# Ordering VectorE and GpSimd work by its room in dry runs, in a hybrid attention and retention layer

## The chip, the cores and the metric

The kernel runs on one core of a Trainium2 chip. The metric is the device time of one execution in microseconds, as the median of the runs taken. Engines are named as in the profile: PE is TensorE (matmuls, with its weight loads as PEld), DVE is VectorE, ACT is ScalarE, POOL is GpSimd, SP is SyncE, which here issues the DMAs. Each engine carries out its own instructions strictly in the order in which the program emits them, and waits on semaphores for the others.

## The reference, cut to what matters

One decoder layer on a sequence of 1024 tokens, model width 1024, float32. Two token mixers read one input projection: retention with 8 heads, in chunks of 128 tokens, and a sparse attention with 8 query heads on one shared key and value, in which an indexer scores all earlier keys for each query and keeps the best 256. Their outputs go through one output projection; a gated convolutional MLP (inner width 2816) follows.

```python
def reference(x, ...):
    hn = rms_norm(h, mix_norm_pre[l])
    proj = hn @ w_in[l]
    rq, rk, rv, rg, aq, ak, av, iq, ik, iw = split_columns(proj)
    ...
    ret_out = retention(rq, rk, rv, rg)
    ...
    att_out = dsa_attention(aq, ak, av, iq, ik, iw)
    mixed = jnp.concatenate([ret_out, att_out], axis=-1) @ w_out[l]
    h = h + rms_norm(mixed, mix_norm_post[l])
    hn = rms_norm(h, ffn_norm_pre[l])
    up = causal_dwconv(hn @ w_up[l], conv_w[l], conv_b[l])
    g, u = jnp.split(up, 2, axis=-1)
    ffn = (jax.nn.silu(g) * u) @ w_down[l]
    h = h + rms_norm(ffn, ffn_norm_post[l])
```

## The kernel before, in words

The sequence is cut into eight query tiles of 128 tokens (t, or block b in attention). Every float32 matrix product is made of three matmuls on rounded halves: an operand is split into a high half (a cast, mostly on ScalarE) and a low half (a subtraction on VectorE or GpSimd). Up and down projection use a scheme of seven block products in place of eight, numbered i = 0, 1, ..., with operands that are sums of blocks.

What sets the order is a planner inside the program. Each piece of work is a generator (a task) that yields operations, events to wait for, and requests for buffers; the class `Flow` steps them. `Lane` stands for an engine and estimates an operation's length (`cost`), and how long VectorE and GpSimd hold the SBUF port that they share (`port`). `Flow.run` (L308) takes the engine on which some waiting operation can start first, and on that engine the operation with the smallest estimated start plus patience times priority (patience 0 for PE, 0.02 for ScalarE, 0.001 for VectorE, 0.005 for GpSimd); ties go to the smaller priority number. Where an operation may run on several engines, the one that ends it first by the estimates takes it. The operation is emitted at once, so the planner's order is the program's order on each engine. `Store` hands out buffers (pages, PSUM banks) in the same estimated time.

```python
    def run(self):
        ...
            for k in self.live:
                op = k.ops[0] if len(k.ops) == 1 else min(k.ops, key=lambda o: self.start(k, o) + o.us + o.lane.bias)
                ways.append((self.start(k, op), k.prio, k.seq, k, op))
            lane = min(ways, key=lambda w: w[:3])[4].lane
            start, _, _, k, op = min((w for w in ways if w[4].lane is lane),
                                     key=lambda w: (w[0] + lane.patience * w[1], w[1], w[2]))
            self.live.remove(k)
            op.emit()
```

The tasks that matter here, in the program's order. `projections` (L873) runs the input projection's columns over pairs of tiles; each finished tile of columns 0 to 3 starts a `ret_unit` (L902, retention for two heads and one tile: rotations on GpSimd, small matmuls, decay on VectorE), the last column starts `aq_post` (L994, the rotation of the attention queries, on GpSimd) and `att_queries` (L1007). `search` (L801) finds each query's threshold by bisection, followed by a selection chain on VectorE (compare, scan, multiply) for each tile. `att_pair` (L1049) makes a block's logits for two heads; `softmax` (L1078) takes maximum (VectorE), exponential (ScalarE), reciprocal (VectorE or GpSimd) and scaling (GpSimd, ScalarE or VectorE); then PE transposes the probabilities and multiplies them with the values. `w_split` (L483) splits weights of the output projection, whose matmuls are `mix0` and `mix1`; `mix1_post` (L1171), `hn_part` (L1233) and `hn_pair` (L1244) normalise its result and prepare sums of blocks for the up projection, `up_first` (L1309) and `up_sums` (L1334) its first operands. In the down projection `dn_split` (L1525, priority 25) splits the operands (product i, step k, side j) and `dn_sums` (L1563, priority 24) makes the sums that products 2, 3 and 5 need. All matmuls are recorded at L437, transposes at L447, loads at L407.

## Time and profile before

| | us |
|---|---|
| median of 3 runs (1332.53 to 1333.96) | 1333.94 |
| the profiled execution | 1332.06 |
| its span | 1330.3 |
| TensorE busy | 1256.3 |
| VectorE busy | 1085.3 |
| ScalarE busy | 715.9 |
| GpSimd busy | 362.8 |

The profiled execution took 1332.06 us, of which 1330.3 are the span, from the first to the last instruction on the profile; the other 1.8 lie around it. The mean granted clock of TensorE is 0.983 of full speed. Busy time is what instructions of an engine covered; waiting inside the span is the rest. The views used below are tables of busy time by window and timelines of one engine, in which the idle time ahead of an instruction stands in brackets with what ended it.

### The profile page before, as it was taken

The page shows a single profiled execution, that of the slowest core. Times are in us where ns is not written, and L with a number is a line of the kernel's source. Part 1 is how long each engine was busy: PE and PEld are TensorE (multiplying, and loading weights), DVE is VectorE, ACT ScalarE, POOL GpSimd, SP SyncE. Part 2 cuts the span into 40 slices and gives each one's busy share as a digit, 9 for nine tenths or more (in the row PEclk, how much of TensorE's full clock was granted, in tenths as well). Part 3 has the DMA queues.
Part 4 walks back from the last instruction along what each step waited for, and adds up shares of the span by engine and source line. Part 5 has one row for each costly group of instructions (what it writes and reads, how often), then busy time and mean ns, then how long its engine had stood idle before and what let it go on. Part 6 is the DMA issues. An engine that isn't in the chain of part 4 may idle for free.

```text
span 1330.3 us, 17741 instructions
## 1 busy us (share of the span) xinstructions
PE 1256.3 (94%) x6058; PEld 1031.2 (78%) x6058; DVE 1085.3 (82%) x1968; ACT 715.9 (54%) x1511; POOL 362.8 (27%) x524
## 2 busy tenths in 40 slices
PE   8899999999987999999799999999999999899997
PEld 6787888888865888887577787777787778678876
DVE  7895898898888888858889987787787677896766
ACT  6685687787546778844445544434444435344440
POOL 4864475675798323114300000000000000000001
PEclk9999999999998999999899999999999999899999
DMA  7100010120202000033213332222121329542335
GB/s 239 48 17 24 8 57 25 40 58 8 68 0 64 1 1 14 28 142 111 96 50 133 102 96 78 65 95 80 64 95 64 103 68 357 201 143 79 119 117 192
DMA packets 54811, 111.47 MB, mean 84 GB/s; under 512 B 6592, under 2 KB 8256, under 8 KB 54720
## 3 DMA queue, kind: packets, MB, share of 16 engines
q1 hardware_dynamic: 54720, 110.33, 24.9%
q8 instruction: 48, 0.79, 0.3%
q14 instruction: 43, 0.35, 0.1%
HBM read 90.38 MB, written 19.92 MB: 83 GB/s over the span
## 4 chain that ended last, share of the span: by engine, by line
PE 75%; DVE 9%; POOL 7%; ACT 4%; issue 3%; DMA 2%; SPq 0%; DVEq 0%; POOLq 0%; ACTq 0%
PE big L437 38%; PE bank L437 34%; DVE page L136 4%; POOL wide L136 4%; PE bank L447 3%; DVE wide L136 3%; ACT page L136 2%; DVE BIG L136 1%; POOL sms L136 1%; ACT wide L136 1%; PE big L447 1%; POOL page L136 0%; DMA wide<-in_w_dn 0%; DMA wide<-glu_scratch 0%; POOL osq L136 0%
## 5 line engine op out<-in xcount | busy, mean ns | idle before, releaser
L437 PE MATMUL big<-page,BIG 128*128 128x512 f32 x984 | 256.4, 406 | 1.2 <-DVE BIG L136 1.0
L136 DVE TENSOR_TENSOR page<-page,page 128x512 fp32r<-128x512 f32 (+3 forms) x321 | 220.2, 719 | 15.6 <-ACT page L136 12.8
L437 PEld LDWEIGHTS big<-page,BIG 128*128 128x128 f32 x984 | 180.8, 189 | 36.9 <-DVE BIG L136 1.2
L437 PE MATMUL big<-page,page 128*128 128x512 f32 (+4 forms) x797 | 191.8, 376 | 15.1 <-DVE page L136 9.4
L437 PEld LDWEIGHTS big<-page,page 128*128 128x128 f32 x797 | 140.9, 189 | 46.2 <-DVE page L136 11.3
L437 PE MATMUL bank<-page,page 128*128 128x512 f32 (+1 forms) x767 | 168.0, 363 | 2.5 <-ACT ajunk L136 1.3
L437 PE MATMUL bank<-page,BIG 128*128 128x512 f32 (+2 forms) x696 | 156.9, 371 | 3.9 <-DVE BIG L136 2.0
L437 PEld LDWEIGHTS bank<-page,page 128*128 128x128 f32 x767 | 132.4, 192 | 25.1 <-DVE page L136 1.9
L136 POOL TENSOR_SCALAR ss<-ss 128x1 f32<-128x1 f32 x8 | 4.2, 519 | 501.6 <-ACT ajunk L136 501.2
L437 PE MATMUL big<-BIG,page 128*128 128x512 f32 x516 | 131.4, 403 | 9.9 <-ACT page L136 4.7
L437 PEld LDWEIGHTS bank<-page,BIG 128*128 128x128 f32 x696 | 119.8, 197 | 20.8 <-ACT BIG L136 3.1
L437 PE MATMUL bank<-BIG,page 128*128 128x512 f32 x540 | 132.6, 395 | 0.0
L437 PEld LDWEIGHTS big<-BIG,page 128*128 128x128 f32 x516 | 97.3, 191 | 38.0 <-ACT page L136 7.8
L136 DVE SCALAR_TENSOR_TENSOR page<-page,convp,page 128x1023 f32<-128x1023 f32 x86 | 110.0, 1280 | 13.5 <-ACT page L136 12.6
L437 PEld LDWEIGHTS bank<-BIG,page 128*128 128x128 f32 x540 | 101.0, 188 | 24.2
L136 DVE TENSOR_SCALAR_CACHE_REDUCE wide<-page,cand 128x384 bf16<-128x384 f32 (+5 forms) x136 | 111.5, 820 | 2.8
L136 ACT CAST page<-page 128x512 fp32r<-128x512 f32 x146 | 87.3, 619 | 42.2 <-PE bank L437 12.5
L136 POOL TENSOR_TENSOR wide<-wide,page 128x128 f32<-128x128 f32 (+3 forms) x153 | 105.1, 709 | 15.7 <-ACT wide L136 13.5
L136 ACT ACTIVATE page<-page,convp 128x1024 f32<-128x1024 f32 x43 | 53.5, 1244 | 90.4 <-PE big L437 38.2
L437 PE MATMUL big<-wide,page 128*128 128x512 f32 x396 | 96.3, 391 | 1.5 <-DVE page L136 0.8
L437 PE MATMUL bank<-wide,page 128*128 128x512 f32 x396 | 95.9, 391 | 0.0
L136 DVE TENSOR_TENSOR page<-bank,page 128x512 fp32r<-128x512 f32 (+3 forms) x111 | 70.5, 638 | 29.2 <-PE bank L437 16.1
(184 smaller groups left out, 2003.7 us busy)
## 6 DMA issues: line engine op xcount, KB each, us to landing
page<-in_w_up SPq DMA_DIRECT2D x88, 256.0 KB, 3.3
glu_scratch<-page SPq DMA_DIRECT2D x21, 512.0 KB, 2.9
wide<-in_w_main SPq DMA_DIRECT2D x40, 256.0 KB, 2.7
wide<-glu_scratch SPq DMA_DIRECT2D x26, 256.0 KB, 5.4
BIG<-glu_scratch SPq DMA_DIRECT2D x25, 256.0 KB, 3.4
BIG<-in_w_dn SPq DMA_DIRECT2D x24, 256.0 KB, 3.9
wide<-in_w_dn SPq DMA_DIRECT2D x22, 256.0 KB, 5.8
page<-in_w_dn SPq DMA_DIRECT2D x20, 256.0 KB, 3.9
```

The costliest lines, as they stand in the source:

```text
L136: return lambda *a, **kw: Op(self, self.cost(m, a, kw), lambda: f(*a, **kw), port=self.port(m, a, kw))
L437: x = nc.tensor.matmul(o, l, r, start=st, stop=sp_, skip_group_check=more)
L447: x = nc.tensor.transpose(tr[:, j * P:(j + 1) * P], s, ident)
```

## The change

The program now plans its order up to twelve times without emitting anything, and emits the order of the best. Each dry run logs every operation with its start, its engine, its end, the operations on which it depends and a key that names it in every run. `Flow.latest` goes back from the end and gives each operation the latest moment at which it can start without delaying what depends on it or the next operation of PE. In the following run `Flow.rank` takes the place of patience times priority on VectorE and GpSimd: an operation's room is its latest moment minus its present start, and what is added to the start in the comparison is 0.3 us for 30 us of room or more, and less in proportion below that. The plan handed on is the mean of the last one and the new one. In the order that comes out as best, a plan is in use; it holds the same operations as before.

Two estimates are corrected: a matmul whose moving operand is in the buffer `BIG` counts 2195 columns for each us in place of 2240, and the scan on VectorE now holds the port that VectorE and GpSimd share. Since tasks may now overtake each other, some buffers are given back only after more events (`att_end`, `up_rest`, `mix1_post`, the rotation table, the controller).

```diff
+PASSES = 12
...
-        if self.name != "dve" or "accum_out" in kw or m in ("memset", "tensor_tensor_reduce", "tensor_tensor_scan"):
+        if self.name != "dve" or "accum_out" in kw or m in ("memset", "tensor_tensor_reduce"):
...
+    def rank(self, lane, w):
+
+
+        if not self.plan or lane.name not in ("dve", "pool"):
+            return lane.patience * w[1]
+        room = self.plan.get(w[3].key + (-1, w[3].calls), w[0] + 20.0) - w[0]
+        return 0.3 * min(1.0, max(0.0, room / 30.0))
+
+    def latest(self):
+
+        end = max(r[2] for r in self.log)
+        late = [end] * len(self.log)
+        after = end
+        for n in sorted(range(len(self.log)), key=lambda n: -self.log[n][0]):
+            start, lane, ready, deps, _ = self.log[n]
+            x = min(late[n], after) if lane == "pe" else late[n]
+            late[n] = x = x - (ready - start)
+            if lane == "pe":
+                after = x
+            for d in deps:
+                late[d] = min(late[d], x)
+        return {r[4]: late[n] for n, r in enumerate(self.log)}
...
-                                     key=lambda w: (w[0] + lane.patience * w[1], w[1], w[2]))
+                                     key=lambda w: (w[0] + self.rank(lane, w), w[1], w[2]))
             self.live.remove(k)
-            op.emit()
+            if not self.dry:
+                op.emit()
...
+            n = len(self.log)
+            self.log.append((start, op.lane.name, k.ready, k.deps, k.key + (-1, k.calls)))
+            k.calls += 1
+            k.deps = (n,)
...
-            us += max(0.11, n / 2240) if r.dtype == F32R else 2 * max(0.107, n / 1200) + 0.0053
+            us += max(0.11, n / (2195 if "BIG" in str(r.name) else 2240)) if r.dtype == F32R else 2 * max(0.107, n / 1200) + 0.0053
...
+        flow.set(turned[c, t])
...
+        if b in (3, 5):
+            yield R_ev[3, T - 1]
...
-        if t == T - 1:
+        left[0] -= 1
+        if not left[0]:
             mem.put(gp, g2)
...
+                yield ev[2]
...
-        for e in aq_ev:
+        for e in aq_ev + list(turned.values()):
...
-        yield att_ev[T - 1]
+        for e in att_ev:
+            yield e
...
+    if dry:
+        raise Ordered(flow, not any(s.queue for s in (mem, acc, bigs)))
...
+    def build(plan, dry):
+        nc = _bacc.Bacc("TRN2", target_bir_lowering=False, num_devices=1, dynamic_dma_scratch_size=1024)
+        io = {k: nc.dram_tensor(f"in_{k}", v.shape, mybir.dt.from_np(v.dtype), kind="ExternalInput").ap()
+              for k, v in arrays.items()}
+        out = nc.dram_tensor("out_0", (S, D), F32, kind="ExternalOutput").ap()
+        with tile.TileContext(nc) as tc:
+            hybrid_layer(tc, io, out, plan, dry)
+        return nc
+
+    best, plan, ends = {}, {}, []
+    for i in range(PASSES):
+        try:
+            build(plan, True)
+        except Ordered as run:
+            if not run.whole:
+                break
+            end = max(r[2] for r in run.flow.log)
+            if not ends or end < min(ends):
+                best = plan
+            ends.append(end)
+            late = run.flow.latest()
+            plan = {k: 0.5 * (plan.get(k, t) + t) for k, t in late.items()}
+    nc = build(best, False)
```

How it moves instructions is shown at three pieces. The first is TensorE, in attention, up to the transposes of the probabilities of block 1, heads 4 and 5. In these rows `ident` is the identity of a transpose, `page_394` and `page_395` hold keys (the matmuls on them are logits), matmuls with `BIG` in groups of three are steps of a projection or of `mix0`. Before (the transposes of heads 4 and 5 are the last two rows):

```order
L437 MATMUL big_4024<-page_395,page_3677 128x256
L447 MATMUL bank_4021<-ident,wide_91 128x128 x4
L447 MATMUL bank_4056<-ident,page_4002 128x128 x4
L447 MATMUL bank_4063<-ident,wide_91 128x128 x4
L447 MATMUL bank_4066<-ident,page_4002 128x128 x4
L437 MATMUL bank_4057<-page_4030,page_296 128x256 x4
L437 MATMUL big_4085<-page_394,page_4001 128x384
L437 MATMUL big_4085<-page_395,page_4001 128x384
L437 MATMUL big_4090<-page_394,page_4001 128x384
L437 MATMUL big_4090<-page_395,page_4001 128x384
L447 MATMUL bank_4125<-ident,wide_91 128x128
L447 MATMUL bank_4125<-ident,page_3958 128x128
```

After (the transposes of heads 4 and 5 are again the last two rows):

```order
L485 MATMUL big_3957<-page_394,page_3669 128x256
L485 MATMUL big_3957<-page_395,page_3669 128x256
L485 MATMUL big_3921<-page_2859,BIG 128x512 x3
L485 MATMUL bank_3968<-page_3422,BIG 128x512 x3
L485 MATMUL big_3921<-page_3294,BIG 128x512 x6
L485 MATMUL big_3921<-page_3311,BIG 128x512 x6
L495 MATMUL bank_4000<-ident,wide_91 128x128 x4
L485 MATMUL big_4013<-page_394,page_3899 128x384
L485 MATMUL big_4013<-page_395,page_3899 128x384
L485 MATMUL big_3921<-page_3325,BIG 128x512 x6
L495 MATMUL bank_4026<-ident,page_3887 128x128
L495 MATMUL bank_4026<-ident,page_3888 128x128
```

Ahead of these transposes now stand seven projection steps and one of `mix0` (x3 is one step, x6 two), where before the last projection step lay further up and only transposes and attention's own matmuls stood; the logits of block 2 come one pair instead of two ahead of them.

The second piece is VectorE in the same place. ISA with `mxs` is the maximum of a softmax and the read of its accumulator; SCALAR_TENSOR_TENSOR with `wide` alone is the selection's scan. Before (block 1, head 4 is the maximum on `big_3959`; the scan is that of tile 7):

```order
L136 TENSOR_SCALAR wide_91<-page_1291,cand 128x1024
L136 TENSOR_TENSOR page_3895<-wide_89,page_3895 128x512
L136 SCALAR_TENSOR_TENSOR wide_89<-wide_91 128x1024
L136 SCALAR_TENSOR_TENSOR wide_91<-wide_89,cnt,wide_91 128x1024
L136 TENSOR_TENSOR page_3957<-bank_3951,page_3957 128x256
L136 ISA wide_91,mxs<-big_3959,wide_89 128x256
L136 ISA mxs 128x1
L136 SCALAR_TENSOR_TENSOR page_1291<-page_1291,cand,wide_91 128x1024
```

After (head 4 is the maximum on `big_3897`, heads 5 to 7 those that follow; the scan is that of tile 6, and the RECIPROCAL is head 4's):

```order
L138 ISA page_3887,mxs<-big_3897,wide_89 128x256
L138 ISA mxs 128x1
L138 TENSOR_TENSOR page_3913<-bank_3891,page_3913 128x512
L138 ISA page_3888,mxs<-big_3907,wide_89 128x256
...
L138 ISA wide_89,mxs<-big_3938,wide_89 128x256
...
L138 ISA wide_91,mxs<-big_3957,wide_89 128x256
...
L138 SCALAR_TENSOR_TENSOR wide_91<-wide_90 128x896
L138 RECIPROCAL sms<-sms 128x1
```

The scan of tile 7 and the selection around it stood ahead of head 4's maximum; now the maxima of all of block 1 stand ahead of tile 6's scan, and tile 7's comes later still. Head 4's reciprocal, which was on GpSimd behind the rotations of tiles 6 and 7, follows the scan of tile 6 on VectorE.

The third piece is VectorE at the start of the down projection, around the low halves of product 0, steps 9 and 10. Before, these are the rows on `page4_9591` and `page5_9613` (step 9) and `page12_9637` and `page7_9640` (step 10); those on `page6_9614` and `page20_9636` belong to product 1, and the rest are `dn_sums`:

```order
L136 TENSOR_TENSOR BIG_9369<-page14_8946,page0_9048 128x512
L136 TENSOR_TENSOR page0_9048<-wide0_9366,page11_9046 128x512
L136 TENSOR_TENSOR BIG_9369<-BIG_9369,page15_8801 128x512
L136 TENSOR_TENSOR page4_9591<-wide2_9368,page4_9591 128x512
L136 TENSOR_TENSOR BIG_9369<-BIG_9369 128x512
L136 TENSOR_TENSOR page5_9613<-wide2_9368,page5_9613 128x512
L136 TENSOR_TENSOR page15_8801<-page15_8801,wide0_9366 128x512
L136 TENSOR_TENSOR page6_9614<-wide2_9368,page6_9614 128x512
L136 TENSOR_TENSOR page0_9048<-BIG_9369,page14_8946 128x512
L136 TENSOR_TENSOR page20_9636<-wide2_9368,page20_9636 128x512
L136 TENSOR_TENSOR page12_9637<-wide1_9367,page12_9637 128x512
L136 TENSOR_TENSOR page7_9640<-wide1_9367,page7_9640 128x512
```

After, they are the rows on `page17_9608` and `page0_9630` (step 9) and `page12_9653` and `page1_9661` (step 10):

```order
L138 TENSOR_TENSOR BIG_9385<-page1_9392,page20_8955 128x512
L138 TENSOR_TENSOR page17_9608<-wide1_9383,page17_9608 128x512
L138 TENSOR_TENSOR BIG_9385<-BIG_9385,page20_8955 128x512
L138 TENSOR_TENSOR BIG_9385<-wide0_9382 128x512
L138 TENSOR_TENSOR BIG_9385<-page1_9392,BIG_9385 128x512
L138 TENSOR_TENSOR page0_9630<-wide1_9383,page0_9630 128x512
L138 TENSOR_TENSOR page20_8955<-page20_8955,page13_9386 128x512
L138 TENSOR_TENSOR BIG_9385<-wide1_9383,page5_8813 128x512
L138 TENSOR_TENSOR page20_8955<-page1_9392 128x512
L138 TENSOR_TENSOR BIG_9385<-BIG_9385,page8_8814 128x512
L138 TENSOR_TENSOR page12_9653<-wide0_9382,page12_9653 128x512
L138 TENSOR_TENSOR page1_9661<-wide0_9382,page1_9661 128x512
```

The sums among these rows are now those of steps 0 and 1 and before were those of steps 2 and 3: the four low halves have moved ahead of most of `dn_sums`.

## Rows read from the trace of the kernel before

**Rows 1.** The page, part 1: each engine's busy time, its share of the span, and its instructions.

```profile
PE 1256.3 (94%) x6058; PEld 1031.2 (78%) x6058; DVE 1085.3 (82%) x1968; ACT 715.9 (54%) x1511; POOL 362.8 (27%) x524
```

**Rows 2.** Busy time by stage, a table of windows of the span: the stretch (us from the span's start), its length, then for TensorE (PE), its weight loads (PEld), VectorE (DVE), ScalarE (ACT) and GpSimd (POOL) the busy us and in brackets the instructions, TensorE's granted clock as a share of full speed, the DMA engines' share, GB/s.

```profile
150.00:350.00 200.00, 199.46 (x1006) 166.73 (x1005) 181.37 (x526) 153.92 (x456) 131.59 (x238) 1.00 0.14 40
350.00:450.00 100.00, 84.75 (x442) 67.93 (x442) 85.79 (x166) 53.15 (x142) 75.93 (x74) 0.95 0.09 26
450.00:575.00 125.00, 117.62 (x769) 102.85 (x768) 105.57 (x213) 96.28 (x193) 31.44 (x38) 1.00 0.04 12
575.00:655.00 80.00, 70.63 (x330) 56.78 (x329) 59.69 (x91) 32.82 (x69) 27.17 (x44) 0.94 0.40 140
655.00:1090.00 435.00, 424.49 (x1839) 339.84 (x1838) 352.05 (x477) 192.66 (x274) 0.74 (x2) 1.00 0.25 82
1090.00:1180.00 90.00, 82.00 (x338) 66.06 (x337) 75.83 (x121) 35.29 (x64) 2.24 (x4) 0.94 0.62 216
```

**Rows 3.** TensorE's timeline where attention begins. In this and all timelines below: start in us, length in us, engine, line, operation, out<-in by the program's names with the tile's shape, xcount of like instructions in a row, and in square brackets the idle time just before them with what ended it.

```profile
413.93 0.86 PE L437 MATMUL big<-page,BIG 128*128 128x512 f32 x3
...
418.37 0.63 PE L447 MATMUL bank<-ident,wide 128*128 128x128 f32 x4 [1.49 <-issue]
...
419.75 0.86 PE L437 MATMUL big<-page,page 128*128 128x384 f32 x4
427.46 0.48 PE L447 MATMUL bank<-ident,wide 128*128 128x128 f32 x1 [6.84 <-ACT wide L136]
...
428.61 1.63 PE L437 MATMUL big<-page,page 128*128 128x384 f32 x4
```

**Rows 4.** VectorE's timeline in the same place. Line L136 is the helper through which all VectorE, ScalarE and GpSimd operations are recorded. TENSOR_TENSOR_SCAN is the scan of the selection for query tile 7; the custom instruction at 410.80 is the maximum of block 1, head 4; the four sums at 421.82 are low halves of `w_split` and `att_queries`.

```profile
405.84 3.38 DVE L136 TENSOR_TENSOR_SCAN wide<-wide 128x1024 f32<-128x1024 bf16 x1
409.26 1.28 DVE L136 SCALAR_TENSOR_TENSOR wide<-wide,cnt,wide 128x1024 bf16<-128x1024 f32 x1
...
410.80 0.41 DVE L136 CUSTOM_DVE_ANT_0 wide<-big,wide 128x256 f32<-128x256 f32 x1
...
421.82 4.63 DVE L136 TENSOR_TENSOR page<-wide,page 128x512 fp32r<-128x512 f32 x4
```

**Rows 5.** ScalarE's timeline in the same place: the exponential of block 1, head 4.

```profile
417.53 0.52 ACT L136 ACTIVATE wide<-wide,mxs 128x256 f32<-128x256 f32 x1
```

**Rows 6.** GpSimd's timeline in the same place: a product of 512 columns, two reciprocals of block 1 (`sms`), the rotations of `aq_post` for tiles 6 and 7, and the reciprocals of block 1's heads 4 to 6 and of one head of block 2.

```profile
401.50 1.30 POOL L136 TENSOR_TENSOR wide<-wide,page 128x512 f32<-128x512 f32 x1
...
407.04 3.91 POOL L136 TENSOR_TENSOR sms<-sms,consts 128x1 f32<-128x1 f32 x2
...
415.65 6.21 POOL L136 TENSOR_TENSOR wide<-wide,page 128x256 f32<-128x256 f32 x6 [0.97 <-ACT wide L136]
421.82 2.40 POOL L136 TENSOR_TENSOR wide<-wide 128x512 f32<-128x512 f32 x1
424.19 1.71 POOL L136 TENSOR_TENSOR wide<-wide,wide 128x512 f32<-128x512 f32 x1
425.87 2.62 POOL L136 TENSOR_TENSOR sms<-sms,consts 128x1 f32<-128x1 f32 x4
```

**Rows 7.** TensorE's granted clock (the column PEclk, ahead of the DMA share) in two short windows of the same table as Rows 2.

```profile
420.00:432.00 12.00, 5.03 (x21) 4.10 (x20) 9.56 (x21) 7.54 (x20) 8.49 (x8) 0.72 0.32 92
...
1141.00:1149.00 8.00, 6.61 (x17) 5.22 (x18) 8.00 (x15) 0.94 (x2) 0.00 (x0) 0.57 0.83 269
```

**Rows 8.** TensorE's timeline at the start of the down projection. The matmuls up to 1143.41 are the last of product 0 there (its steps 9 and 10), the one at 1171.07 opens step 3 of product 3.

```profile
1135.19 1.75 PE L437 MATMUL big<-page,page 128*128 128x512 f32 x7
1138.78 0.96 PE L437 MATMUL big<-page,page 128*128 128x512 f32 x3 [1.84 <-DVE page L136]
1142.39 1.22 PE L437 MATMUL big<-page,page 128*128 128x512 f32 x2 [2.65 <-DVE page L136]
1143.41 10.67 PE L437 MATMUL bank<-page,page 128*128 128x512 f32 x36
...
1171.07 0.73 PE L437 MATMUL big<-page,page 128*128 128x512 f32 x2 [2.73 <-DVE page L136]
1171.64 8.64 PE L437 MATMUL bank<-page,page 128*128 128x512 f32 x30
```

**Rows 9.** TensorE's timeline later in the down projection, 36 such matmuls in a stretch of granted clock 1.00.

```profile
1242.30 8.32 PE L437 MATMUL big<-page,page 128*128 128x512 f32 x36
```

**Rows 10.** VectorE's timeline at the start of the down projection: the first of `dn_sums`, the low half of step 9's first operand, the five low halves of steps 9 and 10 that follow one another, and the next operation after a wait.

```profile
1122.38 0.69 DVE L136 TENSOR_TENSOR BIG<-page,page 128x512 f32<-128x512 f32 x1 [1.19 <-DMA page<-glu_scratch]
...
1136.84 0.68 DVE L136 TENSOR_TENSOR page<-wide,page 128x512 fp32r<-128x512 f32 x1
...
1140.45 3.09 DVE L136 TENSOR_TENSOR page<-wide,page 128x512 fp32r<-128x512 f32 x5
...
1152.73 1.29 DVE L136 TENSOR_TENSOR page<-BIG,page 128x512 fp32r<-128x512 f32 x2 [3.17 <-ACT page L136]
```

**Rows 11.** ScalarE's timeline in the same place: the last high half of product 0 (step 10, second operand).

```profile
1129.12 0.62 ACT L136 CAST page<-wide 128x512 fp32r<-128x512 f32 x1 [0.75 <-DVE page L136]
```

**Rows 12.** SyncE's DMA issues in the same place: the loads of `dn_2` for step 4.

```profile
1140.56 0.80 SPq L407 DMA_DIRECT2D BIG<-glu_scratch  x2
```

**Rows 13.** TensorE's timeline at the end of the output projection: the transposes of tile 6, first half, and the first matmuls that need a sum of `hn_part`.

```profile
644.35 1.11 PE L447 MATMUL big<-ident,page 128*128 128x128 f32 x4 [4.94 <-DVE page L136]
...
647.90 5.49 PE L437 MATMUL big<-BIG,page 128*128 128x512 f32 x12 [1.17 <-DVE BIG L136]
```

More of the change, by code (lines that the diff above doesn't have):

```diff
@@ L59, in __init__ @@
     def __init__(self):
-        self.t, self.val, self.waiters, self.last = None, None, [], ""
+        self.t, self.val, self.waiters, self.last, self.deps = None, None, [], "", ()
 class Want:
@@ L145, in __init__ @@
         self.pages = [(0.0, i) for i in range(n)]
+        self.deps = {}
         self.halves, self.split = [], {}
@@ L194, in put @@
             self.used[b.kind] -= 1
+            i = b.page if isinstance(b.page, int) else b.page[0]
+            old = self.deps.get(i, ()) if not isinstance(b.page, int) else ()
+            self.deps[i] = tuple(set(old[-6:] + tuple(self.flow.cur.deps)))
             if isinstance(b.page, int):
@@ L256, in __init__ @@
         self.port = {"dve": 0.0, "pool": 0.0}
+        self.log, self.plan, self.dry = [], {}, False
     def spawn(self, gen, prio=None):
@@ L261, in spawn @@
         if self.cur is not None:
-            k.last = self.cur.last
+            k.last, k.deps, k.key = self.cur.last, self.cur.deps, self.cur.key + (self.cur.kids,)
+            self.cur.kids += 1
+        else:
+            k.key = (self.seq,)
         self.woken.append((k, None))
@@ L266, in set, with wake @@
     def set(self, ev, val=None):
-        ev.t, ev.val, ev.last = self.now, val, self.cur.last
+        ev.t, ev.val, ev.last, ev.deps = self.now, val, self.cur.last, self.cur.deps
         for k in ev.waiters:
-            self.wake(k, ev.t, val, ev.last)
-    def wake(self, k, t, val, last=""):
+            self.wake(k, ev.t, val, ev.last, ev.deps)
+    def wake(self, k, t, val, last="", deps=()):
         if t > k.ready:
             k.ready, k.last = t, last
+        k.deps = tuple(set(k.deps + tuple(deps)))
         self.woken.append((k, val))
@@ L290, in step @@
                     k.ready, k.last = x.t, x.last
+                k.deps = tuple(set(k.deps + tuple(x.deps)))
                 val = x.val
@@ L330, in run, with __init__ @@
                 k.ready, k.last = op.lane.free, op.lane.name
+            n = len(self.log)
+            self.log.append((start, op.lane.name, k.ready, k.deps, k.key + (-1, k.calls)))
+            k.calls += 1
+            k.deps = (n,)
             self.step(k, None)
+class Ordered(Exception):
+    def __init__(self, flow, whole):
+        self.flow, self.whole = flow, whole
 def isoff(t):
@@ L338, in hybrid_layer @@
 @with_exitstack
-def hybrid_layer(ctx: ExitStack, tc: tile.TileContext, io, out):
+def hybrid_layer(ctx: ExitStack, tc: tile.TileContext, io, out, plan, dry):
     nc = tc.nc
@@ L345, in hybrid_layer @@
     flow = Flow()
+    flow.plan, flow.dry = plan, dry
     pe, act, dve, pool, sp = (Lane(n, e) for n, e in (("pe", nc.tensor), ("act", nc.scalar), ("dve", nc.vector),
@@ L870, in hybrid_layer @@
     row_ev, aq_ev, ret_ev, q_ev = ([Event() for _ in range(T)] for _ in range(4))
-    ro, aqp = {}, {}
+    turned = {(c, t): Event() for c in range(4) for t in range(T)}
+    ro = {}
     def projections():
@@ L1169, in x_again @@
         flow.set(shared["xres", t], b)
+    left = [T]
     def mix1_post(t, ps):
@@ L1891 @@
     arrays = {k: np.ascontiguousarray(v) for k, v in arrays.items()}
-    nc = _bacc.Bacc("TRN2", target_bir_lowering=False, num_devices=1, dynamic_dma_scratch_size=1024)
-    io = {k: nc.dram_tensor(f"in_{k}", v.shape, mybir.dt.from_np(v.dtype), kind="ExternalInput").ap()
-          for k, v in arrays.items()}
-    out = nc.dram_tensor("out_0", (S, D), F32, kind="ExternalOutput").ap()
-    with tile.TileContext(nc) as tc:
-        hybrid_layer(tc, io, out)
+    def build(plan, dry):
[20 more added lines that the diff above has]
+    nc = build(best, False)
     r = _run(nc, [{f"in_{k}": v for k, v in arrays.items()}], core_ids=[0])
```

7 lines of the change are left out of this document (4 added, 3 removed).

## The prediction

> **What bounds the kernel now.** The page comes first: TensorE (PE) is busy for 1256.3 us of the 1330.3 us span [rows 1]. An order of VectorE and GpSimd operations adds no work to PE and takes none away, so it can win only PE's 74 us of idle time and the time that PE loses at half clock, and it can lose by new waits. The view of busy time by stage says where the idle time is [rows 2]: 15.3 us of 350 to 450 (attention begins, the projections end), 9.4 of 575 to 655 (output projection), 8.0 of 1090 to 1180 (start of the down projection), 7.4 of 450 to 575, 10.5 spread over the 435 us of the up projection, and only 0.5 of 150 to 350, where retention runs beside projections; the first 150 us and the last 150 hold the rest. The timelines then show what a long wait waited for.
>
> **Attention, 350 to 450.** PE ends the last step of the projections that fill gaps here at 414.79, and then waits 1.49 us at 418.37 and 6.84 us at 427.46, where it transposes the probabilities of block 1, head 4 [rows 3]. The head's chain: its maximum on VectorE at 410.80, its exponential on ScalarE at 417.53, its reciprocal on GpSimd at 425.87, and its scaling on ScalarE comes after that [rows 4 to 6]. The operations themselves take 0.41 + 0.52 + 0.65 us and a scaling of about the exponential's length; out of 427.46 - 410.80 = 16.7 us some 14 are queueing. VectorE is in the selection of query tile 7 just then (one scan takes 3.38 us), and GpSimd does the rotations of `aq_post` for tiles 6 and 7, 6.21 + 2.40 + 1.71 = 10.3 us, ahead of the reciprocal [rows 4, 6]. The four 384-column matmuls that took 0.86 us at 419.75 take 1.63 at 428.61 [rows 3], and the granted clock of that window is 0.72 [rows 7]: the idle time is followed by work at the lower level, 1.2 GHz.
>
> The change moves the selection of tiles 6 and 7 behind block 1's maxima (its scan stands behind those of heads 4 to 7), puts head 4's reciprocal on VectorE, right behind the scan of tile 6, and lets the rotations of tiles 6 and 7 follow block 2's softmax on GpSimd. On PE eight projection steps of three matmuls remain for after the transposes; at 8.32 us for 36 [rows 9] they are 24 x 0.231 = 5.5 us, less one `mix0` step that comes ahead (0.7). Without its waits PE reached the transposes at 427.46 - 8.33 = 419.1; now it reaches them at about 414.3. Supply: the scan and the selection's next operation, 3.38 + 1.28 = 4.7 us of VectorE [rows 4], no longer stand right ahead of the maximum (410.80 becomes about 406); from there I allow 7 us, half of the queueing that the trace shows: 413. So the 8.3 us close if the queues are no longer than that, and 3 us come back if they are 4 longer. I take 1.5 back. The half clock after the hole goes too; from 0.86 against 1.63 over the 4 us from 427.5 it costs about 1.7 (the four matmuls alone 0.77). Term: -(8.3 + 1.7 - 1.5) = **-8.5**. Ends: -4, if half of the hole comes back, and -13, if the stage's smaller waits close as well. 450 to 575 I leave at 0: the same operations, in another order, with waits of about 1 us each.
>
> Here the trace shows engines holding each other up: the four VectorE sums at 421.82 take 4.63 us beside GpSimd's 2.40 and 1.71, where such sums alone go at one per 0.60, and GpSimd's two reciprocals take 3.91 us beside the scan, where four take 2.62 at 425.87 [rows 4, 6, 10]. The Trainium skill (SBUF — State Buffer, Who interferes with whom) states that a VectorE instruction with two SBUF inputs and a GpSimd instruction that reads SBUF take a port pair as an exclusive lock, and the later one blocks fully; these rows agree with it. The change puts four operations of `w_split` and three of `att_queries` on GpSimd in this stage (1.30 us for such a product [rows 6]). By that rule each could block VectorE for its whole length, 7 x 1.3 = 9 us, which would take back the 8.5; by the rows only part is lost, 4.63 - 4 x 0.60 = 2.2 us of VectorE beside 4.1 us of GpSimd. That is the second case below, not the sum.
>
> **Down projection, 1090 to 1180.** PE waits 1.84 us at 1138.78, 2.65 at 1142.39 and 2.73 at 1171.07, each time for VectorE [rows 8]. VectorE is not slow there; it runs without a break from 1122.38 at one operation per 0.60 us ((1136.84 - 1122.38) / 24 [rows 10]). It is the order: `dn_split` of product 0, steps 9 and 10, waits behind 21 sums of `dn_sums` for products that PE reaches much later, because priority 24 goes ahead of 25. Their low halves come at 1136.84 to 1142.3 [rows 10], though ScalarE had made the high halves by 1129.74 [rows 11]. In the new order they are the 4th, 8th, 13th and 14th operation from the first sum on: 1122.4 + 13 x 0.60 + 0.68 = 1130.9 for the last, against PE's need at 1136.9 (1135.19 + 1.75 [rows 8]). Both waits close with 6 us to spare. Step 3 of product 3 moves from the 74th to the 62nd place: 1122.4 + 61 x 0.60 + 0.7 = 1159.7, or 1162.9 with VectorE's present idle 3.17 us (for operand buffers that PE gives back); PE needs it at 1171.07 - 2.73 = 1168.3, less the 7.2 us saved ahead of it: 1161.1. So 0 to 1.8 us of wait stay there; I take 1.2. Clock: the 36 matmuls behind the second wait take 10.67 us, 8.32 at full speed; the two ahead of them 1.22, where three took 0.96, so some 0.4 too long; the 30 behind the third wait 8.64 against 30 x 0.231 = 6.9 [rows 8, 9]; the granted clock is 0.57 over the first of these stretches [rows 7]. That is 2.35 + 0.4 + 1.7 = 4.4 us. Term: -(1.84 + 2.65 + 2.73 + 4.4 - 1.2) = **-10.4**, ends -8 and -12. What the move costs: the sums of steps 0 to 4 come up to nine operations, 5.4 us, later. Behind those of step 3 SyncE's queue holds the loads for step 4, issued at 1140.56 [rows 12]; by the new place of the sum that frees their buffer they go out some 1.8 us later. The 3.17 us of VectorE idle covers that; without this cover it would be 1.8 us, which the lower end holds.
>
> **Output projection, 575 to 655.** PE waits 4.94 us at 644.35 for `mix1_post` of tile 6 and 1.17 at 647.90 for `hn_part` [rows 13]. The new order takes two `up_first` and the `up_sums` away from ahead of these, but three sums come from GpSimd to VectorE, at nearly the same 0.6 to 0.7 us each; the first wait keeps its size but for some 0.4, the second loses its cause. **-1.5**, ends 0 and -2.5.
>
> **The rest.** The waits for buffers and events that the diff adds (`att_end`, `up_rest`, the controller, the gains, the rotation table) only hold back the moment at which a buffer is given to a later task; each such event belongs to work that in the old order had been issued before. They cost nothing in this sum, and up to one 0.5-us load if one decides. The two corrected estimates enter only through the order: 0 by themselves. 50 to 150 has changed PE order but the same waits: 0, ends -2 and +2. In 150 to 350 PE is busy for 199.46 of 200 us, with producers near their due times: any change there can only lose, 0 to 3; I take **+1**. From 655 to 1090 and from 1180 on the waits belong to chains with one order: 0.
>
> **The sum** is -8.5 - 10.4 - 1.5 + 1 = -19.4 us against the profiled execution's 1332.06, which lies 1.9 below the median: 1312.7 there, and 1333.94 - 19.4 = 1314.5 as a median. I say **1314**.
>
> **Rivals.** (a) Both holes close, as summed: 1304 to 1322, where the ends of the two large terms don't all meet. Chance 0.60. (b) Only the down projection closes. Attention's hole turns up 10 to 50 us later, because the seven operations that went to GpSimd hold VectorE by the port or because rotations of tiles 6 and 7 come too late for block 6: 1314 + 8.5 = 1322, up to 1331 if as much again is lost. For it speaks that DVE and POOL are busy for 86 and 76 of the 100 us [rows 2]; against it that GpSimd is busy for 31 of the next 125 us and so has room. 0.18. (c) The order doesn't act: the dry runs could end without a plan, or with moves that in-order queues cancel. The order as built speaks against the first, since operations do move; the second gives 1331 to 1337. 0.09. (d) **Slower.** The mechanism is retention, 150 to 355: 32 `ret_unit`s, each with dependent steps that PE takes between projection matmuls. Room lets a VectorE or GpSimd operation slide to the moment that a dry run thinks just in time, and PE, in order, waits for each that is late on the chip. At 450 to 575's idle share (7.4 of 125) that is 205 x 5.9% = 12 us and still a gain; at 350 to 450's (15.3%) it is 31 us and gives 1314 + 30 = 1344. It decides from 11% of the stage on (22 us; 0.23 us for each of 3 steps of 32 units). For it: VectorE is busy for 181 of these 200 us. Against it: the old order, made by estimates too, lost 0.5. 0.09. (e) More than summed, below 1304: 0.04.
>
> **How the numbers follow.** The forecast is (a)'s. About 0.2%, 2.7 us, is what a measurement of this kernel can tell from no change. Faster holds (a), (b), (e): 0.82; same (c): 0.09; slower (d): 0.09. From 1303 to 1331 lie (a), (b) and the edge of (e), 0.80.
>
> **What would show it.** In the profile after, no PE wait over 1 us at 1130 to 1145 and half-clock windows gone there; product 3's step 3 under 2 us; no wait over 3 us behind block 1's softmax; 150 to 350 still above 198 of 200. A wait of 1 us or more that repeats in 150 to 355 would be (d); new waits in 430 to 575 behind GpSimd would be (b).

## The result and the profile after

The changed kernel takes 1304.28 us (median of 4 runs, 1302.34 to 1305.54) against 1333.47 for the kernel before: a ratio of 0.9781, 95% interval 0.9764 to 0.9798, 29.2 us less. The forecast was 1314, 19.4 us less; the time lies in the range, near its lower end. The profiled execution took 1305.13 us; its span is 1303.3, against 1330.3.

To see where the time went, the spans of both kernels are cut after the same numbers of matmuls (751, 1801, 2953, 3248, 5146, 5555 and 6001 of the 6058 on record), so that each stage holds equal work of TensorE: the matmuls of a stage have the same shapes in both kernels, but for three at the first cut. Lengths in us, of the one profiled execution of each:

| stage | before | after | difference | forecast |
|---|---|---|---|---|
| start | 155.6 | 153.4 | -2.2 | 0 |
| retention and projections | 208.2 | 207.8 | -0.4 | +1 |
| attention | 213.4 | 198.1 | -15.3 | -8.5 |
| output projection | 72.0 | 70.6 | -1.3 | -1.5 |
| up projection | 450.9 | 454.0 | +3.2 | 0 |
| down projection, first part | 106.4 | 93.7 | -12.7 | -10.4 |
| down projection, second part | 103.2 | 103.2 | 0.0 | 0 |
| end | 20.7 | 22.5 | +1.8 | 0 |

The differences add up to -26.9 us, which is what lies between the two profiled executions (1332.06 and 1305.13); the medians are 29.2 apart.

The windows behind the attention, up and first down rows, first of the kernel before (columns as in [rows 2]):

```profile
363.79:577.14 213.35, 191.08 (x1153) 161.70 (x1153) 181.79 (x357) 144.77 (x314) 98.53 (x100) 0.98 0.06 18
649.12:1100.00 450.88, 440.37 (x1899) 352.68 (x1899) 362.44 (x492) 196.67 (x280) 2.40 (x3) 1.00 0.26 83
1100.00:1206.35 106.35, 98.35 (x410) 79.66 (x410) 95.64 (x156) 45.27 (x85) 2.24 (x4) 0.95 0.64 225
```

and of the kernel after:

```profile
361.21:559.26 198.05, 186.44 (x1153) 158.85 (x1153) 174.70 (x355) 145.40 (x319) 95.08 (x93) 1.00 0.05 16
629.90:1083.94 454.04, 441.31 (x1900) 352.83 (x1899) 364.35 (x491) 203.38 (x288) 1.27 (x2) 0.99 0.25 84
1083.94:1177.63 93.69, 93.02 (x411) 76.71 (x410) 88.40 (x147) 41.60 (x79) 35.83 (x4) 1.00 0.63 222
```

In attention TensorE's idle time, the length of the window less its busy time, goes from 22.3 to 11.6 us, and the busy time of the same 1153 matmuls from 191.1 to 186.4, with the granted clock from 0.98 to 1.00. In the first down part idle time goes from 8.0 to 0.7 us and busy time from 98.4 to 93.0, with the clock from 0.95 to 1.00. The window that had the long wait, [rows 7], now has a granted clock of 1.00.

The chain of block 1, head 4, which answers to [rows 3 to 6], in the kernel after: TensorE's timeline,

```profile
403.51 0.27 PE L495 MATMUL bank<-ident,page 128*128 128x128 f32 x1
405.51 0.55 PE L495 MATMUL bank<-ident,page 128*128 128x128 f32 x3 [1.73 <-POOL page L138]
```

VectorE's (maximum, the scan of tile 6, reciprocal),

```profile
393.65 0.41 DVE L138 CUSTOM_DVE_ANT_0 page<-big,wide 128x256 f32<-128x256 f32 x1
...
399.41 3.16 DVE L138 TENSOR_TENSOR_SCAN wide<-wide 128x896 f32<-128x896 bf16 x1
402.49 0.13 DVE L138 RECIPROCAL sms<-sms 128x1 f32<-128x1 f32 x1
```

ScalarE's (exponential and scaling of head 4, exponential of head 5),

```profile
398.70 0.50 ACT L138 ACTIVATE page<-page,mxs 128x256 f32<-128x256 f32 x1
...
402.66 0.51 ACT L138 ACTIVATE page<-page,sms 128x256 f32<-128x256 f32 x1 [2.44 <-DVE sms L138]
403.07 0.49 ACT L138 ACTIVATE page<-page,mxs 128x256 f32<-128x256 f32 x1
```

and GpSimd's (reciprocal and scaling of head 5, then, much later, the first rotation for tile 6):

```profile
403.74 1.03 POOL L138 TENSOR_TENSOR sms<-sms,consts 128x1 f32<-128x1 f32 x1 [3.05 <-ACT page L138]
404.84 0.61 POOL L138 TENSOR_TENSOR page<-page,sms 128x256 f32<-128x256 f32 x1
...
424.59 1.00 POOL L138 TENSOR_TENSOR wide<-wide,page 128x256 f32<-128x256 f32 x1 [0.42 <-ACT wide L138]
```

From the maximum to the transposes it now takes 403.51 - 393.65 = 9.9 us, where it took 16.7. Where 6.84 us were waited, 1.73 are left, and those are for head 5. Its exponential, at 403.07, stood on ScalarE behind head 4's scaling, which had waited 2.44 us for the reciprocal behind the scan of tile 6; then its reciprocal and scaling went over GpSimd. So a scan of the selection still stands in the way. The rotations of tiles 6 and 7, which stood ahead of the reciprocal, begin at 424.59.

At the start of the down projection, in answer to [rows 8], TensorE's timeline has no wait for VectorE in this stretch any more, and 15 matmuls take 3.56 us, at full clock; the 0.68 us that are left are for ScalarE:

```profile
1119.15 2.88 PE L485 MATMUL big<-page,page 128*128 128x512 f32 x12
1121.87 2.88 PE L485 MATMUL bank<-page,page 128*128 128x512 f32 x12
1124.59 3.56 PE L485 MATMUL big<-page,page 128*128 128x512 f32 x15
1128.83 2.34 PE L485 MATMUL big<-page,page 128*128 128x512 f32 x9 [0.68 <-ACT page L138]
```

At the end of the output projection, in answer to [rows 13], both waits are smaller but there:

```profile
625.75 1.09 PE L495 MATMUL bank<-ident,page 128*128 128x128 f32 x4 [4.33 <-DVE page L138]
...
629.11 5.06 PE L485 MATMUL bank<-BIG,page 128*128 128x512 f32 x11 [0.81 <-DVE BIG L138]
```

### The profile page after: what moved, and what is told of

Read it like the earlier page. It is cut to its first block, busy times and chain, and to the rows that moved or that the text cites. A ratio compares the mean times of both kernels' runs of the same rounds, so it can differ in the third digit from the quotient of the medians.

```text
span 1303.3 us, 17722 instructions
## 1 busy us (share of the span) xinstructions
PE 1247.8 (96%) x6058; PEld 1026.6 (79%) x6058; DVE 1088.5 (84%) x1969; ACT 719.5 (55%) x1517; POOL 413.1 (32%) x517
## 4 chain that ended last, share of the span: by engine, by line
PE 83%; DVE 6%; ACT 3%; POOL 3%; issue 2%; DMA 1%; SPq 0%; DVEq 0%; POOLq 0%; ACTq 0%
PE big L485 44%; PE bank L485 35%; PE bank L495 4%; DVE page L138 3%; POOL wide L138 2%; DVE wide L138 2%; ACT page L138 2%; ACT wide L138 1%; DVE BIG L138 1%; DMA wide<-in_w_misc 1%; PE big L495 0%; POOL r L138 0%; ACT L138 0%; SPq L455 0%; ACT ajunk L138 0%
## 5 line engine op out<-in xcount | busy, mean ns | idle before, releaser
L485 PE MATMUL big<-page,BIG 128*128 128x512 f32 x1032 | 269.3, 405 | 4.0 <-DVE wide L138 1.9
L485 PE MATMUL big<-page,page 128*128 128x512 f32 (+4 forms) x863 | 208.1, 375 | 7.5 <-ACT wide L138 1.2
L138 POOL TENSOR_SCALAR ss<-ss 128x1 f32<-128x1 f32 x8 | 51.7, 6467 | 500.2 <-ACT ajunk L138 499.9
L485 PEld LDWEIGHTS big<-page,page 128*128 128x128 f32 x863 | 152.9, 188 | 39.5 <-DVE mxs L138 3.1
L485 PE MATMUL bank<-page,page 128*128 128x512 f32 (+1 forms) x701 | 149.6, 352 | 1.5 <-ACT ajunk L138 0.8
L485 PE MATMUL bank<-page,BIG 128*128 128x512 f32 (+2 forms) x648 | 147.7, 370 | 3.2 <-ACT BIG L138 1.7
L485 PE MATMUL big<-BIG,page 128*128 128x512 f32 x564 | 141.5, 397 | 9.2 <-DVE page L138 5.6
L485 PEld LDWEIGHTS bank<-page,page 128*128 128x128 f32 x701 | 117.0, 188 | 21.3 <-ACT ajunk L138 1.4
L485 PE MATMUL bank<-wide,page 128*128 128x512 f32 x468 | 113.5, 391 | 1.4 <-ACT page L138 1.2
L485 PEld LDWEIGHTS bank<-wide,page 128*128 128x128 f32 x468 | 87.7, 188 | 21.8 <-ACT page L138 1.6
L138 ACT COPY page<-bank 64x128 f32<-64x128 f32 (+2 forms) x124 | 50.7, 409 | 75.0 <-PE bank L485 56.2
```

Of the source, the lines that this page charges most:

```text
L138: return lambda *a, **kw: Op(self, self.cost(m, a, kw), lambda: f(*a, **kw), port=self.port(m, a, kw))
L485: x = nc.tensor.matmul(o, l, r, start=st, stop=sp_, skip_group_check=more)
```

## The experiments

All medians are of 4 or 5 runs; the kernel before ran beside them and had medians of 1332.5 to 1333.8. The stage lengths are cut as above (us), from one profiled execution of each kernel; in some kernels up to eight matmuls have changed sides at the cut behind attention, about 1 us. Executions of one order differ too: split first has the order of the kernel before in all stages ahead of the down projection, and its attention is 2.1 us longer.

| kernel | median | start | retention | attention | output | up | down 1 | down 2 | end |
|---|---|---|---|---|---|---|---|---|---|
| before | 1333.5 | 155.6 | 208.2 | 213.4 | 72.0 | 450.9 | 106.4 | 103.2 | 20.7 |
| the change | 1304.3 | 153.4 | 207.8 | 198.1 | 70.6 | 454.0 | 93.7 | 103.2 | 22.5 |
| estimates only | 1339.9 | 155.9 | 208.2 | 218.7 | 70.4 | 451.7 | 105.5 | 103.2 | 23.8 |
| plan late only | 1326.1 | 154.9 | 208.4 | 219.8 | 70.4 | 449.9 | 93.7 | 103.2 | 24.2 |
| plan early only | 1314.2 | 154.7 | 210.3 | 202.4 | 71.3 | 448.8 | 103.5 | 101.1 | 20.7 |
| plan, old estimates | 1307.1 | 155.9 | 211.3 | 205.2 | 69.4 | 450.1 | 92.8 | 101.1 | 20.4 |
| VectorE ranked only | 1307.8 | 155.1 | 207.2 | 205.1 | 69.5 | 451.4 | 94.2 | 103.2 | 20.3 |
| GpSimd ranked only | 1318.4 | 155.4 | 209.1 | 202.5 | 69.5 | 454.4 | 104.8 | 101.1 | 20.7 |
| split first | 1326.8 | 156.4 | 208.4 | 215.5 | 72.0 | 449.8 | 94.0 | 108.2 | 20.8 |
| softmax first | 1352.8 | 154.9 | 208.3 | 223.9 | 71.3 | 459.3 | 105.7 | 105.3 | 21.1 |
| splits on VectorE | 1306.2 | 149.6 | 210.1 | 205.3 | 69.1 | 460.2 | 92.8 | 101.1 | 20.3 |
| two dry runs | 1319.6 | 157.7 | 208.9 | 205.7 | 71.2 | 456.0 | 94.8 | 105.7 | 20.3 |
| thirty dry runs | 1292.9 | 147.7 | 209.3 | 197.6 | 68.6 | 452.8 | 92.7 | 101.1 | 20.3 |
| ScalarE ranked too | 1305.2 | 146.1 | 207.2 | 202.8 | 70.8 | 460.0 | 93.7 | 103.2 | 20.3 |

**Estimates only.**

```diff
-PASSES = 12
+PASSES = 0
```

> No dry runs: the old rule of patience times priority sets the order, with the two corrected estimates and the added event waits left in. Theory (the order by room brings the gain, 15 us of it in attention and 11.5 at the start of the down projection): 1328 to 1338 us, the waits of 1 to 3 us for dn_split and the long wait of block 1's softmax are still there. Rival (the corrected estimates carry it): 1300 to 1315 us, attention's long wait gone.

1339.86 us, ratio 1.0047 (1.0029 to 1.0064): slower than before. Both long places are there, attention even 5.3 us longer. The rival falls: without the order by room, the corrected estimates lose about 6 us. With the old estimates and no plan the changed program plans the very order of the kernel before, so that the waits that it adds have no part in these 6 us. This kernel is the baseline for what the order brings with these estimates, 1339.9 - 1304.3 = 35.6 us.

**The plan in one half of the program only.**

```diff
-        if not self.plan or lane.name not in ("dve", "pool"):
+        if not self.plan or lane.name not in ("dve", "pool") or w[0] < 700.0:
```

(late only; early only has `w[0] >= 700.0`)

> The plan ranks VectorE and GpSimd only from the planner's 700th microsecond on (up and down projection); ahead of it the old rule holds. Theory: only the down projection's 11.5 us come, 1333.5 - 11.5 = 1322 us (1318 to 1326); TensorE's waits over 1 us between dn_split and the first products are gone, attention keeps its long wait. Rival (the places are not independent: the early order changes what the late one starts from): outside 1318 to 1326 us.

> The plan ranks only up to the planner's 700th microsecond; from there the old rule holds. Theory: everything but the down projection's 11.5 us, 1304.3 + 11.5 = 1316 us (1311 to 1320); the three waits of 1.8 to 2.7 us for dn_split and the half clock behind them are back, attention's long wait is gone. Rival (not independent): outside 1311 to 1320 us.

Late only: 1326.05 us, ratio 0.9943 (0.9927 to 0.9958), at the edge outside what was expected; early only: 1314.21, 0.9854 (0.9837 to 0.9870), as expected. The late plan takes the first down part to 93.7 us, just as the whole change does, and leaves attention at 219.8; the miss of 4 us is the loss by the estimates, which hold there too. The early plan has attention at 202.4 and the first down part at 103.5. Against estimates only, the halves bring 13.8 and 25.7 us, 39.5 together, where the whole brings 35.6: two separate gains, nearly additive.

**The plan with the old estimates.** Both corrected lines are set back.

```diff
-        if self.name != "dve" or "accum_out" in kw or m in ("memset", "tensor_tensor_reduce"):
+        if self.name != "dve" or "accum_out" in kw or m in ("memset", "tensor_tensor_reduce", "tensor_tensor_scan"):
...
-            us += max(0.11, n / (2195 if "BIG" in str(r.name) else 2240)) if r.dtype == F32R else 2 * max(0.107, n / 1200) + 0.0053
+            us += max(0.11, n / 2240) if r.dtype == F32R else 2 * max(0.107, n / 1200) + 0.0053
```

> The plan with both estimates as before (2240 columns for each us everywhere; the scan holds no port). Theory (order by room alone suffices): 1300 to 1312 us. Rival (the plan needs to know that the scan shuts GpSimd out): GpSimd reciprocals again stand beside scans and attention loses half of its gain, 1312 to 1322 us.

1307.13 us, 0.9798 (0.9778 to 0.9817), as the theory expected for the total. Its attention, 205.2, is 7 us longer than the change's, so that about half of the gain there is gone, as the rival had it; from the output projection on, the stages are shorter. The rival's mechanism is not seen: in attention one GpSimd reciprocal, of 0.55 us, runs beside a scan, where in the kernel before four do, and two orders with the corrected estimates (VectorE ranked only, two dry runs) have 205 us there too. The order by room suffices, and whether the estimates help beside it is within what different orders differ by (below).

**One engine ranked only.**

```diff
-        if not self.plan or lane.name not in ("dve", "pool"):
+        if not self.plan or lane.name != "dve":
```

(GpSimd only has `lane.name != "pool"`)

> The plan ranks VectorE only; GpSimd keeps patience times priority. Theory (VectorE's order carries the down projection alone, and attention needs both engines, GpSimd's rotations out of the way of the reciprocals): the down projection's first part 93 to 95 us as in the change, attention about half way between 218.6 (estimates only) and 198 us; 1308 to 1320 us. Rival (VectorE's order is all of it): within 3 us of the change, 1301 to 1307.

> The plan ranks GpSimd only; VectorE keeps patience times priority. Theory: the down projection, where GpSimd has four instructions, keeps its three waits (105 us), attention closes by a part; 1318 to 1332 us. Rival (GpSimd's order does nothing by itself): 1336 to 1343 us, as with the estimates only.

VectorE only: 1307.84 us, 0.9811 (0.9791 to 0.9830), between what theory and rival expected. GpSimd only: 1318.39, 0.9889 (0.9871 to 0.9906), at the near end of what the theory expected. The down projection is VectorE's alone, 94.2 against 104.8 us. Attention isn't half and half: either engine by itself brings 13.5 or 16.2 of the 20.6 us between estimates only and the change. To order one of the two by room is already most of it.

**Two constants in place of the plan**, each one number in the kernel before.

```diff
-        return spawn(dn_split(i, k, j, src, ready), 25)
+        return spawn(dn_split(i, k, j, src, ready), 23)
```

> The kernel before with one number changed: priority 23 in place of 25 for dn_split, ahead of dn_sums (24), no plan, old estimates. Theory (the three waits at the start of the down projection are this order and nothing else): that part falls from 106.3 to 93 to 96 us, the rest as before, 1320 to 1324 us. Rival (sums that come late stall products 2 and 3 instead): over 1326 us, with new waits between 1150 and 1200.

1326.77 us, 0.9962 (0.9947 to 0.9976). The first down part falls to 94.0 us, which shows that its waits were this order and nothing else. But 5.0 us come back in the second part: `dn_split` now always goes first, so sums come late, and TensorE's timeline has new waits there:

```profile
1202.90 0.49 PE L437 MATMUL big<-page,page 128*128 128x512 f32 x1 [2.32 <-ACT page L136]
1204.06 1.22 PE L437 MATMUL big<-page,page 128*128 128x512 f32 x2 [0.66 <-DVE page L136]
1205.08 9.34 PE L437 MATMUL bank<-page,page 128*128 128x512 f32 x36
```

Again the matmuls behind the wait run long (36 in 9.34 us against 8.32 [rows 9]).

```diff
-            hd.append(spawn(softmax(b, 2 * hp + j, zs[j], big, bias), 90))
+            hd.append(spawn(softmax(b, 2 * hp + j, zs[j], big, bias), 2))
```

> The kernel before with one number changed: priority 2 in place of 90 for softmax, ahead of search (19), aq_post (18) and w_split (23), no plan, old estimates. Theory of the prediction (the long wait is queueing of block 1's softmax behind selection, splits and rotations): the 6.8 us wait closes, attention falls from 213.4 to 202 to 207 us, 1322 to 1328 us. Rival (a constant priority only shifts the wait to what is pushed back, room is needed): attention 210 us or more, 1330 us or more.

1352.78 us, 1.0154 (1.0136 to 1.0171): the rival. The wait of 6.84 us is gone, but attention is 10.6 us longer: its idle time is 27.8 us in place of 22.3, in many smaller waits. Part of them is `w_split`, which, now behind every softmax, is late for `mix0` (matmuls of `page` and `BIG`), as TensorE's timeline shows:

```profile
434.42 0.96 PE L437 MATMUL bank<-page,BIG 128*128 128x512 f32 x3 [1.58 <-DVE page L136]
436.12 0.73 PE L437 MATMUL bank<-page,BIG 128*128 128x512 f32 x2 [0.74 <-DVE page L136]
...
438.25 1.72 PE L437 MATMUL bank<-page,BIG 128*128 128x512 f32 x6 [0.44 <-DVE page L136]
...
461.12 0.65 PE L447 MATMUL bank<-ident,wide 128*128 128x128 f32 x4 [2.36 <-DVE page L136]
```

So a constant that moves the same operations forward closes the same wait and opens others; room moves forward only those that TensorE wants soon.

**The splits kept off GpSimd.**

```diff
-        yield from split(w[:, 0], w[:, 1], r.ap[:, :n])
+        yield from split(w[:, 0], w[:, 1], r.ap[:, :n], (dve,) if i >= 40 else (dve, pool))
...
-            yield from split(st[:, :, 0, :], st[:, :, 1, :], heads(a.ap))
+            yield from split(st[:, :, 0, :], st[:, :, 1, :], heads(a.ap), (dve,))
```

> The change, but the low halves of att_queries and of w_split from the 40th on (the output projection's weights) may only be made on VectorE, and the dry runs plan with that. Rival (b) of the prediction (each such product on GpSimd holds the shared port and blocks VectorE for its whole 1.3 us, so taking them away costs VectorE nothing): attention no longer than 198 us, 1299 to 1306 us. Theory (only part is lost, and VectorE, the fuller engine, is relieved): attention 201 to 206 us, 1307 to 1313 us.

1306.24 us, 0.9809 (0.9789 to 0.9829), with attention at 205.3 us: on the theory's side in the stage, between the two in the total. It doesn't help to keep these products off GpSimd. More it doesn't tell, since its dry runs end in another order, and orders differ by as much in this stage.

**Other orders of the same kind.**

```diff
-PASSES = 12
+PASSES = 2
```

(and 30; the last one adds "act" to the engines that `rank` orders)

> The change with two dry runs in place of twelve: the plan of the first one alone. Theory (room in the order is what helps, and one plan already holds most of it): attention under 207 us, the down projection's first part under 96 us, 1304 to 1316 us. Rival (the gain is a lucky pick out of twelve orders): 1320 us or more.

> The change with up to thirty dry runs, out of which a later one is taken as best. By the theory this is another order of the same kind: 1300 to 1308 us. Rival (the pick decides): more than 6 us away from the change's 1304.

> ScalarE is ranked by room too, where it had patience 0.02 times priority. If ScalarE's queue is what is left of attention's waits (a third of block 1's queueing stood there), attention falls under 196 us and the whole to 1297 to 1303 us; if not, the order is of the same kind or worse, 1303 to 1315 us.

Two dry runs: 1319.59 us, 0.9909 (0.9894 to 0.9923). Up to thirty (the 23rd is the last that comes to an end, and the best by the estimate): 1292.88, 0.9707 (0.9691 to 0.9723), faster than both kernels. ScalarE too: 1305.22, 0.9795 (0.9781 to 0.9810). My theory had the first at 1316 at most and the second at 1300 at least, so the rival, that the pick decides, has a part: one plan brings 20 of the 35.6 us, ten more dry runs and the pick among them another 15, a later pick 11 more. How much of this is the pick, and how much that later plans are better, isn't separated. In all three the first down part is 92.7 to 94.8 us and attention 197.6 to 205.7; what the picks differ in is the start (146 to 158), the up projection (453 to 460) and the second down part. The planner's own estimate of the end was 1277.3 us for estimates only, 1258.9 for two dry runs, 1243.9 for the change and 1243.2 for thirty: it puts these steps of 15 us in the right order, and does not see the last 11. Nor does it see that VectorE ranked only, at 1258.3, is 11.8 us faster than two dry runs. To rank ScalarE by room too does not shorten attention; whether ScalarE's queue is part of what is left there, it does not tell, since orders differ by as much.

## Why the prediction was right, and where its sizes were off

**The way and both places** were right: the plan's order, not the estimates (estimates only), brings the time, in attention and at the start of the down projection (late only, early only); no other stage changes by more than 3.2 us. That the total lies in the range has some luck in it. The four stages with a forecast fell by 29.7 us together, against 19.4; the three that I had left at 0 gave 2.8 back, and without these the median would be 1301.5, below the range.

**Attention, forecast -8.5, measured -15.3**, beyond my far end of -13: the term that was mis-sized. The wait itself was well priced. 8.33 us became 1.73, -6.6 against -6.8 with my 1.5 that come back. Two parts were not. The stage's other idle time, which I left at 0, went from 13.9 to 9.9 us (22.3 - 8.33; 11.6 - 1.73): -4. And the busy time of the same matmuls fell by 4.7, where I had 1.7 for the clock, from the 4 us behind one wait. The clock is most of it, not all. Before, 10.2 us of this stage ran at half clock: 6.8 in the window of [rows 7], and 3.4 in this one, behind a wait of 1.92 us at 372.24:

```profile
372.00:377.00 5.00, 4.76 (x19) 3.84 (x20) 2.91 (x3) 1.69 (x3) 3.93 (x3) 0.66 0.01 3
```

TensorE worked for 7.4 of these 10.2 us, which is 3.7 too long; after, the clock is full throughout. The other 1.0 isn't traced. Nor is 4.7 exact, as split first shows, with the same order here and the same 22.3 us of idle time:

```profile
364.81:580.28 215.47, 193.17 (x1153) 164.64 (x1153) 180.13 (x357) 144.58 (x314) 98.80 (x100) 0.95 0.06 18
```

Its busy time is 2.1 us longer than that of the kernel before, at a lower clock. A stage's loss by the clock has to be read from all its low stretches, not from the row behind the longest wait, and is known to some 2 us here. I also timed the chain wrongly: it comes 10 us earlier than I had it (403 in place of 413), but so does TensorE's need (403.5 in place of 414.3), so that the difference held. Of this, 2.6 us are the earlier start of the stage.

**Down projection, forecast -10.4, measured -12.7.** The three waits are gone, idle -7.3; busy time fell by 5.3 where I had 4.4 for the clock (10.2 us at half clock, of which TensorE worked for 9.3: 4.7); the 1.2 us that I left for product 3's step 3 did not come. The loads that go out later cost nothing that can be seen. That the cause of these waits was the order of `dn_split` behind `dn_sums` is shown by the one-number experiment, 94.0 us.

**Output projection, forecast -1.5, measured -1.3**; but the second wait, which I had gone, is still 0.81 of 1.17, so that its cause was not what I named, or not alone. The two waits give 1.0 together; that the stage comes near the forecast is chance.

**The estimates, forecast 0.** Within the change that can't be told from the noise of orders; alone they cost 6 us. I had not weighed that a corrected length reorders the old rule's choices too.

**Not forecast:** +3.2 us in the up projection and +1.8 at the end, -2.2 at the start. With other orders these stages move by as much either way (449 to 460, 20.3 to 24.2, 146 to 158 us). Which operation makes them so wasn't tried and stays open.

**The rivals.** (b), the hole turning up later because of the shared port, falls: attention as a whole is 15.3 us shorter, with 1.73 us at most of a wait left. (c) falls with estimates only, (d) with retention at 207.8 against 208.2 us and 0.15 us of idle time; no kernel here has more than 211.3 there. The median lies 0.3 us inside (a), next to (e).

## What to carry to other kernels

Where engines work strictly in order and one is nearly full, look for waits in which the awaited engine is busy with something that nobody needs yet: there the order by itself is worth time, and with the waits the busy time of the same matmuls fell by about half to three quarters as much again (4.7 beside 10.7 us, 5.3 beside 7.3), most of it by the clock. A constant priority that closes one such wait tends to open others (two of two here); what helped is a rule by the moment at which the result is wanted, taken from a dry run. Such orders scatter by 10 us and more on the chip, which the dry run sees only in part, so several should be timed and the best kept.

## What the runs showed of the hardware that was not expected

A GpSimd operation of 128 x 1 elements took 46.79 us in the changed kernel. The last of four such operations in its GpSimd timeline:

```profile
1141.71 0.42 POOL L138 TENSOR_SCALAR ss<-ss 128x1 f32<-128x1 f32 x1 [1.45 <-ACT ajunk L138]
1145.39 46.79 POOL L138 TENSOR_SCALAR ss<-ss 128x1 f32<-128x1 f32 x1 [3.26 <-ACT ajunk L138]
```

It took 0.35 us in the kernel before (1167.70 there). VectorE's timeline beside it runs without a break; from 1145.01 on no operation of it reads PSUM, until the GpSimd operation ends at 1192.18, within the two casts:

```profile
1143.81 0.68 DVE L138 TENSOR_TENSOR page<-bank,BIG 128x512 f32<-128x512 f32 x1
...
1145.01 0.68 DVE L138 TENSOR_TENSOR page<-BIG 128x512 f32<-128x512 f32 x1
...
1191.71 0.76 DVE L138 CAST page<-page 128x512 fp32r<-128x512 f32 x2
```

VectorE keeps its pitch of 0.60 us all the while. It happens again with the old estimates (56.23 us) and with ScalarE ranked (52.88), to the same operation, and for 11.79 us in three more kernels (estimates only, plan early only, GpSimd ranked only). The Trainium skill (SBUF — State Buffer, Who interferes with whom) has two-input VectorE operations and GpSimd reads take a shared port pair as an exclusive lock; that fits a wait, but by it the wait ends with the VectorE operation that holds the lock, within 0.7 us here, and the measurement decides: GpSimd stood still for some 75 of them. What ends it can be read in part. In the three kernels with 11.79 us, and with ScalarE ranked, the operation ends 0.05 us after VectorE's last operation ahead of a pause of 0.57 to 2.61 us, as here on GpSimd and VectorE with estimates only:

```profile
1171.96 11.79 POOL L138 TENSOR_SCALAR ss<-ss 128x1 f32<-128x1 f32 x1 [1.45 <-ACT ajunk L138]
...
1183.03 0.67 DVE L138 TENSOR_TENSOR wide<-wide,wide 128x512 f32<-128x512 f32 x1
1184.27 0.69 DVE L138 TENSOR_TENSOR page<-BIG,page 128x512 fp32r<-128x512 f32 x1 [0.57 <-ACT page L138]
```

In the changed kernel and with the old estimates it ends 0.05 us after a cast, yet in the changed kernel an earlier cast, at 1175.12, had not ended it; and in the kernel before the operation of 1167.70 came through after one sum of VectorE, with the next sum right behind. So a pause of VectorE lets GpSimd in; what else does stays open. Nobody waits for the result before 1275, so it cost nothing here.
